# A hybrid conv / gated-linear / differential-attention layer in one kernel: convolution taps kept in emitted order and spread over both attentions, two empty steps more between channels, the first weight casts behind the squares, the low-rank weights loaded earlier

## The chip, the cores and the metric

One core of a Trainium2 chip. The metric is the device time of one execution in microseconds; lower is better. TensorE (PE) does the matrix products, VectorE (DVE) and ScalarE (ACT) the elementwise work, GpSimd (POOL) a few small operations and one queue of DMAs, SyncE (SP) issues nearly all other DMAs.

## What the kernel must compute

One layer of a streaming encoder on x of 1024 positions by 1024 channels, in float32:

```
h = rms_norm(x);  z = h @ W_in, split into the inputs of three mixers and three gates
A: u = a * sigmoid(gate); causal depthwise conv, 31 taps, over positions; LayerNorm; silu; @ w_pw
B: gated linear attention, 4 heads: logf = log_sigmoid(f_low @ w_f_up + b_f) / 16, with f_low 16 wide,
   cumulated in chunks of 64; within and across the chunks; rms_norm; * silu(og)
C: differential attention, 8 heads: softmax(q1 k1) - lam * softmax(q2 k2), chunk-causal,
   in blocks of 128 queries; @ v; rms_norm
x += (sigmoid gates on A, B, C) @ W_out;  x += SwiGLU FFN (2816 hidden);  rms_norm
```

## The kernel before

Each float32 product is three products of a faster format: an operand is split into a rounded high part (`wh`, an ACT cast, L121) and the rest (`wl`, a DVE subtraction, L122) by `hilo`, and `mm3` issues three matmuls (L125 to L127). The work runs in stages, one behind the other on PE: *head* (x is read, normalised, transposed into `h`, first two weight units), *blocks* (projections as seven-product block multiplications, until about 400 us), *gla* (attention B, until about 700 us), *diff* (attention C, head by head, until about 1190 us), the convolution's norm and projection, the output projection, the FFN.

The depthwise convolution is DVE work laid beside PE's. For each of 8 channel groups (`ct`), `conv_taps` emits 31 taps into one tile `acc` (128x1024, a single buffer): the first is a multiplication (L400), the others multiply and add (L402). Behind the last tap `acc` is stored to `c_d` by SP and added into a running sum `s_d` by an accumulating DMA on POOL's queue (L408). Because `acc` has one buffer, the first tap of the next channel waits until these two DMAs have read it. The taps' input comes back from memory `u_d`, written by `conv_in` (L413, L414) when a convolution unit of the blocks stage is finished.

What decides the order: the code calls `tick()` between small groups of matmuls (in the blocks stage every 6). A tick adds `TAP_RATE[stage]` to a counter; for each whole number in it `conv_step` advances `conv_taps` by one `yield`. Thus 31 steps are taps, and the `yield` behind the DMAs and the generator's end are steps that emit nothing. Then a scheduler orders each engine's instructions, and it may move one ahead of others on its engine where it takes the engine to be free, unless `tc.keep_in_program_order` holds it.

At the start SP issues x0, the constants, x1 to x3, the parameters, two weight tiles, x4 to x7. `x_scale(t)` squares an x tile on ACT (L323), forms its factor with a small DVE operation (`sm`, L131) and a POOL power (L132), and scales the tile on DVE (L325). `transposed` turns x0 to x3 into `h` (PE transposes L258, an ACT copy L260, a DVE subtraction L261).

`gla_begin` loads the two low-rank weights: `wf` (L449) and `wu3` (L451), casts `wf` into `wfx` (ACT L121 and L457) and multiplies `h` by it on PE (L466); `decay(0)` forms the gates: `fl`, a DVE minimum (L480), two ACT functions, a DVE subtraction (L483), eight DVE scans (L486), a DVE subtraction (L490). In the blocks stage `mix_finish` adds a finished PSUM block to an earlier one (DVE `t`, L937), which frees the bank for PE. In the diff stage `softmax(qb)` does for 128 queries: scores on PE (L686, L687), mask and maximum on DVE (L689 to L693), two exponentials on ACT (L695), then on DVE two reciprocals, a small product and the combination `p` (L700), which PE transposes; by the tables `LAG` and `SPACE` (L67, L68) the transposes stand 3 or 4 steps of a head's plan behind the scores, and the next block's scores 2 or 3 steps behind them.

Of the kernel before, what the change touches and what calls it, by code (L numbers as in the profile page):

```python
# [7 lines left out]
F32 = mybir.dt.float32  # L8
F32R = mybir.dt.float32r
U8 = mybir.dt.uint8  # L10
AF = mybir.ActivationFunctionType
ALU = mybir.AluOpType
# [4 lines left out]
P = 128  # L17
S = 1024
D = 1024
KT = D // P  # L20
NT = S // P
HALF = 512
# [16 lines left out]
P_DW, P_MIX, P_LNG, P_LNB, P_BF, P_GN, P_DN = 0, 248, 256, 264, 272, 276, 278  # L39
# [26 lines left out]
MIX0, MIX1 = 2, 18  # L66
LAG = (3, 3, 3, 3, 4, 4, 4, 4)  # L67
SPACE = (2, 2, 2, 2, 2, 2, 3, 3)  # L68
TAP_RATE = {"head": 0.0, "blocks": 0.42, "gla": 0.5, "diff": 0.72}


def body(nc, tc, I, out):
    x_d, w_d, wf_d, wfup_d, par_d, lq_d, cst_d, msk_d, ffg_d, fng_d = I
    vec, act, pe, pool, sp = nc.vector, nc.scalar, nc.tensor, nc.gpsimd, nc.sync
# [7 lines left out]
    cv = tc.alloc_tile_pool(name="cv", bufs=1)  # L82
    tp = tc.alloc_tile_pool(name="tp", bufs=8)
    sx = tc.alloc_tile_pool(name="sx", bufs=1)
    y2 = lambda name: yp.tile([P, HALF], F32, tag="y2", name=name)
# [25 lines left out]
    def bank():  # L111
        return ps.tile([P, HALF], F32, tag="pb", name="pb", bufs=4)

    def bank2():
        return ps.tile([P, 2 * HALF], F32, tag="sc", name="sc", bufs=2)

    def f(ap):
        return ap.bitcast(F32)

    def hilo(hi, lo, src):  # L120
        act.copy(hi, src)  # L121
        vec.tensor_tensor(out=lo, in0=src, in1=f(hi), op=ALU.subtract)  # L122

    def mm3(o, ah, al, bh, bl, start, stop, more=False):
        pe.matmul(o, ah, bh, start=start, stop=False, skip_group_check=more)  # L125
# [3 lines left out]
    def rstd(dst, ss, n, width):  # L129

        vec.tensor_scalar(out=dst, in0=ss, scalar1=1.0 / n, scalar2=EPS, op0=ALU.mult, op1=ALU.add)  # L131
        pool.tensor_tensor(out=dst, in0=dst, in1=mhalf[:, 0:width], op=ALU.pow)  # L132
# [5 lines left out]
    def raw_half(i, hf):  # L138
        raw = wp.tile([P, 1024], F32, tag="wr", name="wr", bufs=2)
        sp.dma_start(raw, w_d[i, hf])  # L140
        return raw

    def like(ap, src):
        return ap if len(src.shape) == 2 else ap.rearrange("p (k n) -> p k n", k=src.shape[1])

    def operand(src):
        wh = wp.tile([P, HALF], F32R, tag="wh", name="wh", bufs=8)
        wl = wp.tile([P, HALF], F32R, tag="wl", name="wl", bufs=8)
        hilo(like(wh, src), like(wl, src), src)
        return wh, wl  # L150

    def pieces(i):
        w = []
        ready.append(w)
        for hf in range(2):
            raw = raws0[hf] if i == 0 else raw_half(i, hf)
            for q in range(2):
                w.append(operand(raw[:, q * HALF:(q + 1) * HALF]))
                yield

    def wfinish():
        if state["gen"] is not None:
            for _ in state["gen"]:
                pass
            state["gen"] = None
# [7 lines left out]
    def wpiece():  # L173
        if state["gen"] is not None and next(state["gen"], 0) == 0:
            state["gen"] = None
# [50 lines left out]
    def taps(n):  # L226
        clock["conv"] = min(clock["conv"] + n, 2.0)
        while clock["conv"] >= 1.0 and conv_step():
            clock["conv"] -= 1.0

    def tick():
        if clock["now"] % 2 == 0:
            wpiece()
        clock["now"] += 1
        taps(TAP_RATE.get(clock["stage"], 0.5))
        while events and events[0][0] <= clock["now"]:
# [12 lines left out]
    def transposed(src, hh, hl, half, gcol, full=None):  # L249
        for k in range(KT):  # L250
            if half == 0 and k >= 4:
                if k % 2 == 0:
                    pt2 = bank2()
                pt = pt2[:, hs(k % 2)]
            else:
                pt = bank()
            for t in range(4):
                pe.transpose(pt[:, t * P:(t + 1) * P], src[t][:, k * P:(k + 1) * P], ident)  # L258
            g = par[:, gcol + k:gcol + k + 1]
            act.activation(hh[half][k // 4][:, k % 4, :], pt, AF.Copy, scale=g)  # L260
            vec.scalar_tensor_tensor(out=hl[half][k // 4][:, k % 4, :], in0=pt, scalar=g, in1=f(hh[half][k // 4][:, k % 4, :]),  # L261
                                     op0=ALU.mult, op1=ALU.subtract)
            if full is not None:
                full[k] = x2_("hf")
                act.activation(full[k], pt, AF.Copy, scale=g)
            yield k

    def bigset(pool_, tag, name):
        t = {(i, p): [pool_.tile([P, 4, HALF], F32R, tag=tag, name=f"{name}{p}{i}{j}") for j in range(2)]
             for i in range(2) for p in range(2)}  # L270
        return [[t[i, p] for i in range(2)] for p in range(2)]

    def hk(hset, half, k, c=slice(0, HALF)):
        return hset[0][half][k // 4][:, k % 4, c], hset[1][half][k // 4][:, k % 4, c]
# [19 lines left out]
    def hs(half):  # L294
        return slice(half * HALF, (half + 1) * HALF)


    hset = bigset(big, "big", "h")
# [2 lines left out]
    def tblock(name):  # L301
        T[name] = [tp.tile([P, 4, HALF], F32R, tag="tp", name=f"{name}{p}") for p in range(2)]

    xt2 = [tp.tile([P, 2, D], F32, tag="tp", name="xt") for _ in range(NT // 2)]
    xs = [xt2[t // 2][:, t % 2, :] for t in range(NT)]
    junks = tp.tile([P, 2, D], F32, tag="tp", name="junk")
    sp.dma_start(xs[0], x_d[0])
    sp.dma_start(cst, cst_d)
    for t in range(1, 4):
# [10 lines left out]

    def x_scale(t):
        ss, r = sm[:, t:t + 1], sm[:, 8 + t:9 + t]
        act.activation(junks[:, t % 2, :], xs[t], AF.Square, accum_out=ss)  # L323
        rstd(r, ss, D, 1)
        vec.tensor_scalar(out=xs[t], in0=xs[t], scalar1=r, scalar2=None, op0=ALU.mult)  # L325

    for t in range(4):
        x_scale(t)
    for _ in transposed(xs[0:4], *hset, 0, P_MIX):
        pass  # L330
    wfinish()


# [42 lines left out]
    for j in range(2):  # L376
        vec.tensor_tensor(out=lt[:, j * 64:(j + 1) * 64], in0=lq[:, j * 128:j * 128 + 64],
                          in1=lq[:, j * 128 + 64:j * 128 + 128], op=ALU.mult)
# [16 lines left out]
    def conv_taps(ct, up):  # L395
        acc = cv.tile([P, S], F32, tag="acc", name="acc", bufs=1)
        for j in range(TAPS):
            w = par[:, P_DW + ct * TAPS + j:P_DW + ct * TAPS + j + 1]
            if j == 0:
                vec.tensor_scalar(out=acc, in0=up[:, j:j + S], scalar1=w, scalar2=None, op0=ALU.mult)  # L400
            else:
                vec.scalar_tensor_tensor(out=acc, in0=up[:, j:j + S], scalar=w, in1=acc, op0=ALU.mult, op1=ALU.add)  # L402
            yield 1
        sp.dma_start(c_d[ct], acc)
        if ct == 0:
            sp.dma_start(s_d, acc)
        else:
            pool.dma_start(s_d, acc, accum_op=ALU.add)  # L408
        yield 1

    def conv_in(ct, half, sg, o):

# [25 lines left out]
    h2 = lambda name, dt=F32R: mix.tile([P, HALF], dt, tag="h2", name=name, bufs=8)  # L438
    G, C = {}, {}
# [3 lines left out]
    def gla_begin():  # L443
        ws, fl4, zs = q4("ws").bitcast(F32R), q4("fl").bitcast(F32R), q4("zs")
        C.update(wu=ws[0:96, 0:HALF], sst=ws[:, HALF:2 * HALF], fl=[fl4[0:96, hs(i)] for i in range(2)],
                 z2=zs[:, 0:HALF], sf=[zs[:, HALF + i * DV:HALF + (i + 1) * DV] for i in range(2)])
        wf = h2("wf", F32)[:, 0:KT * 16].rearrange("p (k n) -> p k n", k=KT)
        wu3 = h2("wu3", F32)[0:96, :]
        sp.dma_start(wf, wf_d)  # L449
        for j in range(6):  # L450
            sp.dma_start(wu3[16 * j:16 * j + 16, :], wfup_d)  # L451
        vec.memset(C["z2"], 0.0)
        yield 2
        wfx = mix.tile([P, KT, 96], F32R, tag="o4", name="wfx", bufs=2)
        hilo(wfx[:, :, 0:16], wfx[:, :, 16:32], wf)
        for j in range(1, 3):
            act.copy(wfx[:, :, 32 * j:32 * j + 32], f(wfx[:, :, 0:32]))  # L457
        wu, fl = C["wu"], C["fl"]
        act.copy(wu, wu3)
        vec.tensor_tensor(out=wu[64:96], in0=wu3[64:96], in1=f(wu[64:96]), op=ALU.subtract)  # L460
        yield 1
        for half in range(2):
            o = bank()[0:96, :]
            for k in range(KT):
                for p in range(2):
                    pe.matmul(o, wfx[:, k, :], hk(hset, half, k)[p], start=k + p == 0, stop=k + p == KT)  # L466
            act.copy(fl[half], o)
            vec.tensor_tensor(out=fl[half][32:64], in0=o[32:64], in1=f(fl[half][32:64]), op=ALU.subtract)
            yield 1
        yield from decay(0)  # L470
# [493 lines left out]
    NM = MIX1 - MIX0  # L964
# [15 lines left out]
            mb.make()  # L980
    conv_out(1)
    for n, p in order:
        for _ in range(2):
            if len(mb.made) < AHEAD:
                mb.make()
        mb.product(n, p)
        if mb.nxt == len(order) and len(mb.made) < 4 and state["n"] == MIX0:
            state["n"] = MIX1
            wstart()
        mb.after(n, p)  # L990
# [359 lines left out]
```

## Time and profile before

| | us |
|---|---|
| median of 3 runs (2113.55 to 2117.1) | 2115.08 |
| the profiled execution, its own time | 2115.08 |
| its span, first to last instruction | 2113.3 |
| PE busy | 2048.8 (97%) |
| DVE busy | 1447.5 (68%) |
| ACT busy | 892.8 (42%) |
| mean granted TensorE clock | 0.991 |

The profile's own execution is one of the three runs and the median of them; 1.8 us of it lie outside the span. Busy shares are means over the whole span; the stages differ, and the later sections read them stage by stage.

### The profile page before, as it was taken

To read this page: it belongs to the slowest core of one execution; us is meant where nothing else is said; L and a number is where in the kernel's file an instruction comes from. 1 tells how busy PE (TensorE), PEld (TensorE's weight loads), DVE (VectorE), ACT (ScalarE), POOL (GpSimd) and SP (SyncE) were. 2 spreads that over 40 slices of the span, in tenths; PEclk is the share of its full clock that TensorE was granted. 3 is DMA by queue.
4 is the path that set the end of the run, shared out by engine and by line. 5 is a ranking of instruction groups with operands and counts; after the bars stand their busy time and mean duration, and the time that the engine had idled before them with its cause. 6 is when DMAs were issued, how large, how long until landed. Compare 5 with 4: busy or idle time off the path is not lost.

```text
span 2113.3 us, 28321 instructions
## 1 busy us (share of the span) xinstructions
PE 2048.8 (97%) x10796; PEld 1751.7 (83%) x10796; DVE 1447.5 (68%) x2218; ACT 892.8 (42%) x1843; POOL 60.8 (3%) x64
## 2 busy tenths in 40 slices
PE   6999999899999999999999999999999999999998
PEld 4888787688888989898988888998888888888887
DVE  6999898889898555555554465468655555576766
ACT  6434333244453456556565462235433333432112
POOL 0000000000000000000000000000000000000000
PEclk9999999999999999999999999999999999999999
DMA  4232333421223533434332545342322222282111
GB/s 154 76 125 85 109 116 105 128 80 41 90 85 95 145 81 80 103 78 110 76 91 78 205 144 176 110 151 110 120 80 85 75 80 95 77 307 80 60 40 80
DMA packets 88538, 222.27 MB, mean 105 GB/s; under 512 B 10353, under 2 KB 21233, under 8 KB 88401
## 3 DMA queue, kind: packets, MB, share of 16 engines
q1 hardware_dynamic: 85664, 213.64, 31.2%
q0 software_dynamic: 2736, 6.82, 2.0%
q8 instruction: 85, 1.39, 0.3%
q14 instruction: 53, 0.43, 0.1%
HBM read 147.01 MB, written 54.53 MB: 95 GB/s over the span
## 4 chain that ended last, share of the span: by engine, by line
PE 68%; issue 15%; DVE 9%; DMA 3%; ACT 3%; POOL 1%; SPq 0%; DVEq 0%; POOLq 0%; ACTq 0%
PE pb L125 12%; PE pb L126 12%; PE pb L127 12%; PE sc L125 9%; PE sc L126 9%; PE sc L127 9%; DVE acc L402 3%; DMA s_d<-acc 2%; PE pb L722 2%; DVE wl L122 1%; PE sc L686 1%; PE sc L687 1%; POOL rs L132 1%; PE pb L711 1%; POOL sm L132 0%
## 5 line engine op out<-in xcount | busy, mean ns | idle before, releaser
L121 ACT CAST wh<-wr 128x512 fp32r<-128x512 f32 x315 | 193.5, 621 | 397.9 <-DVE x L1259 139.3
L122 DVE TENSOR_TENSOR wl<-wr,wh 128x512 fp32r<-128x512 f32 x315 | 214.0, 689 | 148.7 <-ACT wh L121 147.9
L402 DVE SCALAR_TENSOR_TENSOR acc<-up,par,acc 128x1024 f32<-128x1024 f32 x240 | 307.5, 1281 | 2.2
L125 PE MATMUL pb<-h,wh 128*128 128x512 f32 x704 | 281.4, 400 | 2.0 <-DVE h L261 2.0
L127 PE MATMUL pb<-h,wl 128*128 128x512 f32 x704 | 276.1, 392 | 0.0
L126 PE MATMUL pb<-h,wh 128*128 128x512 f32 x704 | 275.7, 392 | 0.0
L121 ACT CAST wh<-s 128x512 fp32r<-128x512 f32 x152 | 94.4, 621 | 229.9 <-PE sc L126 139.8
L1259 DVE TENSOR_TENSOR x<-x,pb 128x512 f32<-128x512 f32 x176 | 120.4, 685 | 61.4 <-PE pb L127 60.8
L127 PEld LDWEIGHTS pb<-h,wl 128*128 128x128 f32 x704 | 132.6, 188 | 29.0
L125 PEld LDWEIGHTS pb<-h,wh 128*128 128x128 f32 x704 | 132.7, 189 | 26.8 <-DVE h L261 2.2
L126 PEld LDWEIGHTS pb<-h,wh 128*128 128x128 f32 x704 | 132.8, 189 | 24.3 <-issue 0.2
L125 PE MATMUL pb<-wh,h 128*128 128x256 f32 x512 | 149.7, 292 | 0.4 <-DVE knl L122 0.4
L127 PE MATMUL pb<-wh,h 128*128 128x256 f32 x512 | 146.2, 285 | 0.0
L126 PE MATMUL pb<-wl,h 128*128 128x256 f32 x512 | 146.1, 285 | 0.0
L125 PE MATMUL sc<-bT,wh 128*128 128x512 f32 x352 | 137.0, 390 | 0.5 <-ACT bT L121 0.5
L126 PE MATMUL pb<-wl,mh 128*128 128x512 f32 x352 | 136.9, 389 | 0.0
L125 PE MATMUL pb<-wh,mh 128*128 128x512 f32 x352 | 136.9, 389 | 0.0
L127 PE MATMUL pb<-wh,ml 128*128 128x512 f32 x352 | 136.9, 389 | 0.0
L126 PE MATMUL sc<-bT,wh 128*128 128x512 f32 x352 | 136.8, 389 | 0.0
L127 PE MATMUL sc<-bT,wl 128*128 128x512 f32 x352 | 136.6, 389 | 0.0
L122 DVE TENSOR_TENSOR wl<-s,wh 128x512 fp32r<-128x512 f32 x152 | 104.0, 687 | 28.4 <-ACT wh L121 28.2
L125 PE MATMUL sc<-T,wh 128*128 128x512 f32 x256 | 101.6, 397 | 6.6 <-DVE t L937 6.6
(268 smaller groups left out, 4542.5 us busy)
## 6 DMA issues: line engine op xcount, KB each, us to landing
wr<-w_dram SPq DMA_DIRECT2D x176, 512.0 KB, 3.7
m_d<-t SPq DMA_DIRECT2D x44, 256.0 KB, 2.1
mr<-m_d SPq DMA_DIRECT2D x22, 512.0 KB, 5.5
k<-k SPq DMA_DIRECT2D x48, 128.0 KB, 3.2
kl<-kl SPq DMA_DIRECT2D x48, 128.0 KB, 3.0
xt<-x_dram SPq DMA_DIRECT2D x8, 512.0 KB, 8.4
up<-u_d SPq DMA_DIRECT2D x8, 512.0 KB, 5.5
gt_d<-t SPq DMA_DIRECT2D x16, 256.0 KB, 2.0
```

The costliest lines, as they stand in the source:

```text
L121: act.copy(hi, src)
L122: vec.tensor_tensor(out=lo, in0=src, in1=f(hi), op=ALU.subtract)
L125: pe.matmul(o, ah, bh, start=start, stop=False, skip_group_check=more)
L126: pe.matmul(o, ah, bl, start=False, stop=False, skip_group_check=more)
L127: pe.matmul(o, al, bh, start=False, stop=stop, skip_group_check=more)
L132: pool.tensor_tensor(out=dst, in0=dst, in1=mhalf[:, 0:width], op=ALU.pow)
L402: vec.scalar_tensor_tensor(out=acc, in0=up[:, j:j + S], scalar=w, in1=acc, op0=ALU.mult, op1=ALU.add)
L686: pe.matmul(sc[i][:, c], a["q"][i][:, t], a["k"][i][:, c], start=True, stop=False)
L687: pe.matmul(sc[i][:, c], a["q"][i][:, t], a["kl"][i][:, c], start=False, stop=True)
L711: pe.transpose(pt[:, i * P:(i + 1) * P], pd[:, (g0 + i) * P:(g0 + i + 1) * P], ident)
L722: pe.matmul(ov[:, 0:P], parts[k // 4][:, c], a["v"][:, k, :], start=k == 0, stop=k == nk - 1)
L1259: vec.tensor_tensor(out=xx, in0=xx, in1=o, op=ALU.add)
```

## The change

Four things. (1) The tap rates per tick become 0.45 (blocks), 0.45 (gla) and 0.82 (diff), and every tap is held in program order. (2) Behind each channel the generator yields three times where it yielded once. (3) At the start each x tile has a slot of its own, the squares' unused output goes to `acc`'s slot, and the four first weight casts with their subtractions are emitted one by one inside the loop over `transposed`, behind the four squares, and held there. (4) `wf` and `wu3` are loaded into `y2` tiles inside the blocks loop; `gla_begin` loses its loads and the `yield 2` behind them, and the `yield 1` behind the casts becomes `yield 3`.

```diff
-TAP_RATE = {"head": 0.0, "blocks": 0.42, "gla": 0.5, "diff": 0.72}
+TAP_RATE = {"head": 0.0, "blocks": 0.45, "gla": 0.45, "diff": 0.82}
...
-    def hilo(hi, lo, src):
-        act.copy(hi, src)
-        vec.tensor_tensor(out=lo, in0=src, in1=f(hi), op=ALU.subtract)
+    def stay(op):
+        tc.keep_in_program_order(op)
+
+    def hilo(hi, lo, src, pin=False):
+        a = act.copy(hi, src)
+        b = vec.tensor_tensor(out=lo, in0=src, in1=f(hi), op=ALU.subtract)
+        if pin:
+            stay(a)
+            stay(b)
...
-                w.append(operand(raw[:, q * HALF:(q + 1) * HALF]))
+                w.append(operand(raw[:, q * HALF:(q + 1) * HALF], i == 0))
...
-    xt2 = [tp.tile([P, 2, D], F32, tag="tp", name="xt") for _ in range(NT // 2)]
-    xs = [xt2[t // 2][:, t % 2, :] for t in range(NT)]
-    junks = tp.tile([P, 2, D], F32, tag="tp", name="junk")
+    xs = [tp.tile([P, 2, D], F32, tag="tp", name="xt")[:, 0, :] for _ in range(NT)]
+    junk = cv.tile([P, S], F32, tag="acc", name="junk", bufs=1)
...
     for t in range(4):
         x_scale(t)
-    for _ in transposed(xs[0:4], *hset, 0, P_MIX):
-        pass
+    wpiece()
+    for k in transposed(xs[0:4], *hset, 0, P_MIX):
+        if k % 2:
+            wpiece()
     wfinish()
...
+            stay(op)
             yield 1
         sp.dma_start(c_d[ct], acc)
...
-        yield 1
+        for _ in range(3):
+            yield 1
...
-        wf = h2("wf", F32)[:, 0:KT * 16].rearrange("p (k n) -> p k n", k=KT)
-        wu3 = h2("wu3", F32)[0:96, :]
-        sp.dma_start(wf, wf_d)
-        for j in range(6):
-            sp.dma_start(wu3[16 * j:16 * j + 16, :], wfup_d)
+        wf, wu3 = C["wf"], C["wu3"]
         vec.memset(C["z2"], 0.0)
-        yield 2
...
-        yield 1
+        yield 3
         for half in range(2):
...
     for n, p in order:
+        if (n, p) == (NM - 2, 0):
+            C["wf"] = y2("wf")[:, 0:KT * 16].rearrange("p (k n) -> p k n", k=KT)
+            C["wu3"] = y2("wu3")[0:96, :]
+            sp.dma_start(C["wf"], wf_d)
+            for j in range(6):
+                sp.dma_start(C["wu3"][16 * j:16 * j + 16, :], wfup_d)
```

The new lines shift the numbers: L400, L402 of before are L407, L409 after; L122 is L125, L323 is L328, L260 is L266, L700 is L704.

Place one, ACT at the start of the program (`wh` is a weight cast, `junk` a square, `h` the scaled copy of a transposed block). Before:

```order
L121 ACT_TABLE_LOAD
L121 CAST wh<-wr 128x512 x4
L323 ACTIVATE junk,sm<-xt 128x1024 x6
L260 ACTIVATE h_100<-pb,par 128x512 x4
L260 ACTIVATE h_101<-sc,par 128x512 x2
```

The same place in the changed kernel:

```order
L328 ACT_TABLE_LOAD
L328 ACTIVATE junk,sm<-xt 128x1024 x4
L124 CAST wh<-wr 128x512
L266 ACTIVATE h_100<-pb,par 128x512 x2
L124 CAST wh<-wr 128x512
L266 ACTIVATE h_100<-pb,par 128x512 x2
L124 CAST wh<-wr 128x512
L266 ACTIVATE h_101<-sc,par 128x512 x2
L328 ACTIVATE junk,sm<-xt 128x1024 x2
L266 ACTIVATE h_101<-sc,par 128x512
```

The four casts went from ahead of six squares to behind four, one for each pair of `h` copies; the squares of x4 and x5 stand ahead of the last `h` copies.

Place two, DVE in the gla stage, around the second head's decay chain (`t_3510`, later `t_3514`), where before a channel ended and the next began. Before:

```order
L402 SCALAR_TENSOR_TENSOR acc<-up_98,par,acc 128x1024
L122 TENSOR_TENSOR knl<-pb,knh 128x512
L480 TENSOR_SCALAR t_3510<-pb,par 128x512 x2
L400 TENSOR_SCALAR acc<-up_99,par 128x1024
L122 TENSOR_TENSOR vl<-pb,vh 128x512
L402 SCALAR_TENSOR_TENSOR acc<-up_99,par,acc 128x1024 x2
L483 TENSOR_TENSOR t_3510<-t_3510,t_3509 128x1024
L122 TENSOR_TENSOR knl<-pb,knh 128x512
L486 SCALAR_TENSOR_TENSOR t_3509<-cst,t_3510 128x128 x8
```

The same place in the changed kernel:

```order
L409 SCALAR_TENSOR_TENSOR acc<-up_99,par,acc 128x1024
L125 TENSOR_TENSOR wl<-wr,wh 128x512 x2
L125 TENSOR_TENSOR knl<-pb,knh 128x512
L484 TENSOR_SCALAR t_3514<-pb,par 128x512 x2
L125 TENSOR_TENSOR vl<-pb,vh 128x512
L487 TENSOR_TENSOR t_3514<-t_3514,t_3513 128x1024
L125 TENSOR_TENSOR knl<-pb,knh 128x512
L490 SCALAR_TENSOR_TENSOR t_3513<-cst,t_3514 128x128 x8
L494 TENSOR_TENSOR t_3514<-t_3513 128x1024
```

No tap is left inside the chain, and the channel's boundary, three rows wide before, is elsewhere. Of the 248 taps all stood ahead of the first `p` of the diff stage; now 155 do, and 10, 15, 10, 15, 14, 12 and 17 lie in heads 0 to 6 (counted from one head's first `p` to the next head's). Between a channel's last tap and the next first tap there were 3 to 9 DVE instructions; there are 7 to 31.

Place three, DVE in the diff stage, the softmax of a head's last block of queries (`sc` are scores, `st` the row statistics). Before:

```order
L689 MEMSET sc 64x64
L690 TENSOR_REDUCE st<-sc 128x1
L689 MEMSET sc 64x64
L690 TENSOR_REDUCE st<-sc 128x1
L697 RECIPROCAL st<-st 128x2
L698 TENSOR_SCALAR st<-st,lam 128x1
L700 SCALAR_TENSOR_TENSOR p<-sc,st,p 128x1024
```

The same place in the changed kernel:

```order
L409 SCALAR_TENSOR_TENSOR acc<-up_98,par,acc 128x1024
L693 MEMSET sc 64x64 x2
L694 TENSOR_REDUCE st<-sc 128x1 x2
L409 SCALAR_TENSOR_TENSOR acc<-up_98,par,acc 128x1024 x2
L701 RECIPROCAL st<-st 128x2
L702 TENSOR_SCALAR st<-st,lam 128x1
L704 SCALAR_TENSOR_TENSOR p<-sc,st,p 128x1024
```

Three taps now stand in and ahead of the chain that ends in `p`.

## Rows read from the trace of the kernel before

**Rows 1.** The page, busy time, share of the span, instructions of each engine.

```profile
PE 2048.8 (97%) x10796; PEld 1751.7 (83%) x10796; DVE 1447.5 (68%) x2218; ACT 892.8 (42%) x1843; POOL 60.8 (3%) x64
```

**Rows 2.** Waits of PE: tile waited at, releaser: us, times, longest.

```profile
PE pb L258 <- DVE sm L131: 17.7, 3, 17.2
PE sc L125 <- DVE t L937: 6.6, 2, 3.3
PE pb L466 <- ACT wfx L457: 6.5, 1, 6.5
PE sc L125 <- ACT ah L121: 4.1, 1, 4.1
```

**Rows 3.** Waits of DVE, same columns.

```profile
DVE acc L400 <- DMA s_d<-acc: 24.4, 5, 6.7
```

**Rows 4.** Windows: length, busy time (instructions) by engine, granted clock, DMA share.

```profile
100.00:200.00 100.00, 100.00 (x437) 81.39 (x437) 94.85 (x122) 41.19 (x71) 0.00 (x0) 1.00 0.31 103
240.00:404.00 164.00, 157.39 (x673) 127.68 (x672) 147.41 (x178) 58.89 (x102) 1.73 (x2) 0.98 0.34 110
412.00:426.00 14.00, 12.52 (x47) 8.81 (x48) 12.34 (x13) 5.19 (x8) 0.00 (x0) 0.87 0.20 61
426.00:700.00 274.00, 260.17 (x1660) 236.51 (x1659) 245.81 (x325) 121.43 (x253) 16.67 (x10) 0.98 0.26 78
660.00:700.00 40.00, 38.97 (x260) 35.46 (x259) 39.30 (x48) 14.03 (x33) 1.97 (x1) 1.00 0.32 99
720.00:1140.00 420.00, 415.87 (x2636) 372.98 (x2635) 227.73 (x459) 244.84 (x663) 22.34 (x19) 1.00 0.36 90
1020.00:1040.00 20.00, 19.29 (x132) 17.50 (x131) 14.83 (x30) 14.74 (x39) 1.78 (x2) 1.00 0.72 172
```

**Rows 5.** Timeline of DVE, blocks and gla: start, duration, instruction, [idle before].

```profile
241.53 0.75 DVE L400 TENSOR_SCALAR acc<-up,par 128x1024 f32<-128x1024 f32 x1 [3.69 <-DMA s_d<-acc]
...
249.64 0.69 DVE L937 TENSOR_TENSOR t<-sc,c 128x512 f32<-128x512 f32 x1
...
469.52 0.76 DVE L400 TENSOR_SCALAR acc<-up,par 128x1024 f32<-128x1024 f32 x1 [6.68 <-DMA s_d<-acc]
```

**Rows 6.** The page, costliest groups: busy us, mean ns of one, idle.

```profile
L402 DVE SCALAR_TENSOR_TENSOR acc<-up,par,acc 128x1024 f32<-128x1024 f32 x240 | 307.5, 1281 | 2.2
```

**Rows 7.** Line L408, the accumulating DMA, issue to landing.

```profile
DMA to landing us min/median/max: 6.0/8.2/9.0
```

**Rows 8.** Timeline at the start of gla, SP's queue and ACT.

```profile
408.89 0.33 SPq L449 DMA_DIRECT2D wf<-wf_dram  x1
...
410.90 0.30 ACT L121 CAST wfx<-wf 128x128 fp32r<-128x128 f32 x1 [9.93 <-DMA wf<-wf_dram]
```

**Rows 9.** Timelines of ACT, DVE and PE at the start.

```profile
12.07 2.42 ACT L121 CAST wh<-wr 128x512 fp32r<-128x512 f32 x4 [10.05 <-DMA wr<-w_dram]
14.39 1.05 ACT L323 ACTIVATE junk<-xt 128x1024 f32<-128x1024 f32 x1
...
22.15 2.42 ACT L260 ACTIVATE h<-pb,par 128x512 fp32r<-128x512 f32 x4 [1.42 <-PE pb L258]
...
20.83 0.75 DVE L325 TENSOR_SCALAR xt<-xt,sm 128x1024 f32<-128x1024 f32 x1 [0.66 <-POOL sm L132]
...
24.83 1.40 DVE L261 SCALAR_TENSOR_TENSOR h<-pb,par,h 128x512 fp32r<-128x512 f32 x2
...
25.62 0.50 PE L125 MATMUL pb<-h,wh 128*128 128x512 f32 x1 [1.98 <-DVE h L261]
```

**Rows 10.** Line L310, the loads of x1 to x3: issue ns, first and last start.

```profile
L310 SPq DMA_DIRECT2D xt<-x_dram x3: 424/432/432, 1.7 to 2.6; - x3
...
DMA to landing us min/median/max: 6.2/7.0/7.8
```

**Rows 11.** Timeline of POOL around the last tap.

```profile
689.06 1.97 POOL L132 TENSOR_TENSOR rs<-rs,mhalf 128x4 f32<-128x4 f32 x1 [35.87 <-DVE rs L131]
...
709.78 1.03 POOL L132 TENSOR_TENSOR rs<-rs,mhalf 128x4 f32<-128x4 f32 x1 [8.35 <-DVE rs L131]
```

More of the change, by code (lines that the diff above doesn't have):

```diff
@@ L144, in like, with operand @@
         return ap if len(src.shape) == 2 else ap.rearrange("p (k n) -> p k n", k=src.shape[1])
-    def operand(src):
+    def operand(src, pin=False):
         wh = wp.tile([P, HALF], F32R, tag="wh", name="wh", bufs=8)
         wl = wp.tile([P, HALF], F32R, tag="wl", name="wl", bufs=8)
-        hilo(like(wh, src), like(wl, src), src)
+        hilo(like(wh, src), like(wl, src), src, pin)
         return wh, wl
@@ L322, in x_scale @@
         ss, r = sm[:, t:t + 1], sm[:, 8 + t:9 + t]
-        act.activation(junks[:, t % 2, :], xs[t], AF.Square, accum_out=ss)
+        act.activation(junk, xs[t], AF.Square, accum_out=ss)
         rstd(r, ss, D, 1)
@@ L399, in conv_taps @@
             if j == 0:
-                vec.tensor_scalar(out=acc, in0=up[:, j:j + S], scalar1=w, scalar2=None, op0=ALU.mult)
+                op = vec.tensor_scalar(out=acc, in0=up[:, j:j + S], scalar1=w, scalar2=None, op0=ALU.mult)
             else:
-                vec.scalar_tensor_tensor(out=acc, in0=up[:, j:j + S], scalar=w, in1=acc, op0=ALU.mult, op1=ALU.add)
+                op = vec.scalar_tensor_tensor(out=acc, in0=up[:, j:j + S], scalar=w, in1=acc, op0=ALU.mult, op1=ALU.add)
+            stay(op)
             yield 1
```

## The prediction

> **What bounds the kernel now.** I read the page's busy times first: PE works 2048.8 us of a span of 2113.3 [rows 1], so 64.5 us are idle, and only these, with what the clock loses behind them, can be won by moving other engines' work. The list of PE's waits says where they lie [rows 2]: 17.7 us at the first transposes, 6.6 us in two waits for `t` in the blocks stage, 6.5 us for `wfx` at the start of gla, 4.1 us for `ah` in gla. In DVE's list one wait stands out: the first tap of a channel waits for the accumulating DMA, 24.4 us in five times [rows 3]. The timeline joins them [rows 5]: at 241.53 the first tap had held DVE idle for 3.69 us; DVE, in order, was then behind, and the `t` that PE needed came at 249.64, when PE had waited 3.3 us.
>
> The windows price each stage [rows 4]. From 100 to 200 us DVE is 94.85% busy and PE loses nothing: a full DVE costs nothing by itself while it is not late. From 240 to 404 us PE lacks 164 - 157.39 = 6.6 us and the granted clock is 0.98, which is another 0.02 x 164 = 3.3: **9.9 us**. From 404 to 426 us it lacks 6.5 for `wfx` and 14 - 12.52 = 1.5, and the clock at 0.87 over 14 us is 1.8 more: **9.8 us**. From 426 to 700 us it lacks 13.8, the clock at 0.98 is 5.5 more: **19.3 us**. From 720 to 1140 us it lacks 4.1 in 420.
>
> **The start.** Today ACT stands before its first cast until the weights land at 12.07; four casts, and the first square begins at 14.39 although x1 to x3 had all landed by 2.6 + 7.8 = 10.4 [rows 10]; the fourth tile is scaled at 20.83 and the first real matmul runs at 25.62 [rows 9]. In the new order the squares come first. The last tile is there at 10.4; a square takes 1.05 us [rows 9], with its read-out I put 1.2, so 11.6. On DVE the scaling of x2 and three small parameter operations stand ahead of x3's factor, which I put at 12.3; the wait for the power and the scaling were 0.66 and 0.75 us [rows 9], with the factor's small operation ahead 1.6, so x3 is scaled at 13.9. Before, ACT's first copy began 22.15 - (20.83 + 0.75) = 0.6 behind the scaling; then 0.6 for the copy (2.42 / 4), 0.7 for DVE's part (1.40 / 2) and little more: first matmul at about 15.9, a gain of at most 9.7 us. Not all of it stays. The copies for the second half of `h` come behind three casts, and the squares of x4 and x5 stand ahead of the last of them (two times 1.04 us), so PE, which needs 12 matmuls of about 100/437 = 0.23 us [rows 4] for the first half, runs dry once more, by 2 to 3 us. I take **-7.5** (bounds -4 and -9.7).
>
> **Blocks.** A tap is 1.28 us [rows 6]. The accumulating DMA lands 6.0 to 9.0 us after its issue [rows 7]. A tick is 6 matmuls, 1.4 us; from the step that issues the DMA to the next first tap there were 2 steps at 0.42 a tick, 2 / 0.42 x 1.4 = 6.7 us on paper, and the scheduler moved taps ahead of that. Now there are 4 at 0.45, 12 us, and taps stay. The effective rate hardly moves: 0.42 x 31/33 = 0.394 taps a tick before, 0.45 x 31/35 = 0.399 after, so DVE is as full as in the clean window. The price is the spacing alone, and DVE fills it with weight subtractions. I take **-9** of 9.9; one boundary has only seven DVE instructions in it, which at 0.7 us are 4.8 and leave 1 to 4 us of wait that DVE may or may not catch up (bounds -5 and -9.9).
>
> **Start of gla.** The issue of `wf` came at 408.89 and its cast at 410.90, so the load itself is 2.0 us on PE's way [rows 8]; SP stood before it behind a store of `u_d`, which waits for DVE's `t`, which was late behind a first tap. With the loads moved into the blocks stage, SP passes them long before, and the casts hang only on room in the pool and DVE. Two ticks of slack are added between the casts and their matmuls, and two removed before them, so PE's own order does not change much. Seven small DMAs stand on SP's queue earlier, about 3 us of issue, where it has room (DMA share 0.31, rows 4, at 100 to 200 us). I take **-7** of 9.8 (bounds -2, the load alone, and -9.8).
>
> **The rest of gla.** The largest term. Before, 248 taps stood ahead of diff's first `p`; now 155. Four channels, 124 taps, are through by the end of blocks in both, so gla keeps 31 of 124, and DVE's 245.8 us of 274 [rows 4] fall by 93 x 1.28 = 119 to about 127, under half. The waits of 4.1 us for `ah` (behind the first tap that waited 6.68 us, rows 5) and those behind decay chains mixed with taps should go. What stays is the chain's own length: eight scans, three subtractions and four ACT functions. I take **-14** of 19.3 (bounds -8 and -18).
>
> **Diff, the price.** The 93 taps land in heads 0 to 6, 119 us on DVE, whose 227.7 us of 420 become 347, 83%. The densest window has 14.83 of 20 [rows 4]; with its share, 5.7 us, it is full. Inside a softmax one to four taps delay `p` by 1.3 to 5.1 us, while PE has 3 or 4 steps of the head's plan to work on before it needs `p`. What a full DVE costs in an attention stage shows at 660 to 700 us: 39.30 of 40 busy with 20 taps in it, and PE lacks 1.0 us [rows 4]. The dense part is about half of each head; 7 heads at 0.5 us give **+3.5** (bounds 0 and, at one stall like that of 241 us in each head, 3.3 + 1.7 of clock, 7 x 5 = 35).
>
> A rule speaks against this part. Rows first: POOL's power `rs` on a 128x4 tile took 1.97 us among taps and 1.03 just behind the last one [rows 11], so taps slow POOL by 0.9 us each time. In diff one such power per head would cost 7 x 0.9 = 6 us if PE waited for it; it is consumed a head later, so I put nothing. The Trainium skill ("SBUF — State Buffer", section "Who interferes with whom") says that VectorE and GpSimd hold a shared port pair exclusively and the later one blocks; the trace agrees in direction, and by that rule with nothing to hide behind the sum would be 6 us worse, 2087.
>
> **Sum.** -7.5 - 9 - 7 - 14 + 3.5 = -34. The profiled execution's own time is 2115.08, which is also the median: **2081 us**.
>
> **Rivals.** *The stalls move to diff.* Softmax is a chain through DVE, ACT and DVE, and a tap of 1.28 us is longer than most of its links. For it: the dense windows become full, and taps no longer give way. Against it: 660 to 700 us. At one stall of 5 us in every second head the time is 2081 - 3.5 + 17 = 2095; at one in each head 2112, no change.
>
> *Slower than before.* The same mechanism twice a head: both dense blocks late, PE idle 3.3 and the clock 1.7 each time, 14 x 5 = 70 against 37.5 saved: 2148. It decides from 7.5 stalls on (one per head and a little). Against it: DVE keeps 17% free over the stretch.
>
> *The wait only moves.* The first taps after boundaries inside gla and diff still meet the DMA, and `wfx` still waits for the stores of `u_d`; the start gives 4. Then -4 - 6 - 2 - 10 + 3.5 = -18.5: 2097. For it: seven DVE instructions at one boundary, 7.7 us of landing on average.
>
> *More than forecast.* All bounds at their best: -9.7 - 9.9 - 9.8 - 18 = -47: 2068.
>
> **Chances.** Forecast (2072 to 2090) 0.60; better than that 0.10; the wait only moves 0.14; stalls in some heads 0.07; stalls in each, no change, 0.04; slower 0.05. The 80% range goes from 2066, the best case, to 2101, past the wait that moves and the stalls in half the heads. About 0.2% (4.2 us) is what a measurement can tell from no change: faster 0.91, same 0.04, slower 0.05.
>
> **What would show it.** First matmul near 16 us and a short second gap by 25; no idle of PE from 100 to 400 us and clock 1.00 there; the first taps' wait for the DMA under 8 us in all; `wfx` cast not waiting for a load; DVE about half busy in the gla stage and PE idle there under 6 us; from 720 to 1140 DVE near 347 us and PE idle 4 to 10. Wrong it would be if PE's list shows waits for `p` of more than 2 us per head with clock under 1.00, or if the first tap's wait stays above 15 us.

## The result

The changed kernel takes 2077.95 us (median of 4 runs, 2076.41 to 2080.82) against 2116.09 for the kernel before in the same comparison: the ratio of the means is 0.9823, 95% interval 0.9806 to 0.984. The forecast was 2081 us. The page of the changed kernel gives the busy times:

```profile
PE 2034.9 (98%) x10796; PEld 1741.6 (84%) x10796; DVE 1445.1 (70%) x2218; ACT 890.3 (43%) x1843; POOL 56.3 (3%) x64
```

The span is 2074.6 us, so PE idles 39.7 us where it idled 64.5 [rows 1]; its busy time fell by 13.9 us with the same 10796 matmuls; the mean granted clock rose from 0.991 to 0.999. PE's list of waits, the answer to [rows 2]:

```profile
PE pb L264 <- DVE xt L330: 10.4, 3, 9.6
PE sc L690 <- ACT p L699: 8.7, 4, 2.2
PE sc L690 <- DVE p L704: 1.6, 1, 1.6
...
PE sc L690 <- ACT osb L727: 1.4, 1, 1.4
...
PE pb L470 <- ACT wfx L461: 0.6, 1, 0.6
```

The waits for `t` and `ah` are nearly or quite gone, that for `wfx` fell from 6.5 to 0.6 us. The waits for `sc` in the diff stage grew: six waits, 11.7 us, where there had been six of 3.7 us together, by these lines of the kernel before:

```profile
PE sc L686 <- DVE p L700: 1.9, 3, 0.7
PE sc L686 <- ACT jk L725: 1.3, 2, 0.6
PE sc L686 <- ACT wh L121: 0.5, 1, 0.5
```

In DVE's list the first taps' wait for the accumulating DMA fell from 24.4 us [rows 3] to:

```profile
DVE acc L407 <- DMA s_d<-acc: 2.2, 1, 2.2
```

The windows that answer to [rows 4], cut where the same matmuls stand in the changed kernel (columns as there; 240 to 404, 404 to 426, 426 to 700 and 720 to 1140 us before):

```profile
233.84:387.77 153.93, 153.93 (x672) 125.25 (x671) 121.22 (x155) 59.12 (x102) 1.94 (x2) 1.00 0.37 117
387.77:402.57 14.80, 12.94 (x55) 9.13 (x54) 4.87 (x8) 6.12 (x10) 0.00 (x0) 1.00 0.16 50
402.57:654.37 251.80, 251.47 (x1660) 230.91 (x1659) 177.78 (x264) 122.07 (x255) 9.00 (x8) 1.00 0.25 75
674.06:1101.66 427.60, 415.89 (x2635) 372.38 (x2634) 332.42 (x553) 241.70 (x663) 25.90 (x23) 1.00 0.40 100
```

The four stretches took 164, 22, 274 and 420 us before; they take 153.9, 14.8, 251.8 and 427.6. In blocks PE lacks nothing and in gla 0.3 us, at clock 1.00; in diff it lacks 11.7 us where it lacked 4.1. DVE, 90% busy in the first and the third before (147.41 of 164, 245.81 of 274), is at 79% and 71%; in diff it rose from 54% to 78%. The rest of the span from diff's last matmul on is unchanged (933.9 us before, 933.6 after).

For each run the trace gives the starts of four matmul lines, and so the length of each stage. By the line numbers of the kernel before, the first is the first product (L125), the second the low-rank product (L466, so the wait for `wfx` counts to the stage ahead of it), the third the first scores (L686), the fourth the last of L722; all in us, of the profiled execution, with the measured ratio of all runs:

| kernel | first product | to gla | gla | diff | ratio to before |
|---|---|---|---|---|---|
| before | 25.6 | 386.7 | 313.9 | 453.2 | 1 |
| changed | 16.5 | 373.2 | 290.5 | 460.8 | 0.9823 |
| start as before | 26.1 | 370.8 | 290.6 | 463.9 | 0.9856 |
| one yield | 17.1 | 373.0 | 291.9 | 460.3 | 0.9825 |
| taps not held | 15.9 | 387.4 | 315.6 | 453.3 | 0.9955 |
| weights loaded in gla | 16.2 | 374.2 | 290.1 | 463.9 | 0.9827 |
| no taps in diff | 17.4 | 373.0 | 290.4 | 453.1 | 0.9764 |
| gla 0.60, diff 0.64 | 16.6 | 373.4 | 295.9 | 466.2 | 0.9846 |
| old rates | 16.0 | 372.1 | 296.8 | 470.2 | 0.9861 |
| before, taps held | 25.7 | 372.4 | 295.6 | 466.4 | 0.9893 |
| changed, again | 16.1 | 373.6 | 290.6 | 460.9 | 0.9817 |
| blocks 0.60 | 17.1 | 391.5 | 293.2 | 464.1 | 0.9912 |
| pause in each head | 16.9 | 373.1 | 291.4 | 456.8 | 0.9792 |
| both | 16.0 | 389.1 | 292.1 | 454.5 | 0.9864 |

### The profile page after: what moved, and what is told of

Read it like the earlier page. It is cut to its first block, busy times and chain, and to the rows that moved or that the text cites. A ratio compares the mean times of both kernels' runs of the same rounds, so it can differ in the third digit from the quotient of the medians.

```text
span 2074.6 us, 28309 instructions
## 1 busy us (share of the span) xinstructions
PE 2034.9 (98%) x10796; PEld 1741.6 (84%) x10796; DVE 1445.1 (70%) x2218; ACT 890.3 (43%) x1843; POOL 56.3 (3%) x64
## 4 chain that ended last, share of the span: by engine, by line
PE 79%; issue 9%; DVE 7%; ACT 2%; DMA 1%; POOL 1%; SPq 0%; DVEq 0%; POOLq 0%; ACTq 0%
PE pb L131 15%; PE pb L132 15%; PE pb L133 15%; PE sc L131 10%; PE sc L132 9%; PE sc L133 9%; PE pb L726 2%; DVE acc L409 1%; PE sc L690 1%; DVE wl L125 1%; PE sc L691 1%; PE pb L715 1%; DMA wr<-w_dram 1%; POOL sm L138 0%; POOL rs L138 0%
## 5 line engine op out<-in xcount | busy, mean ns | idle before, releaser
L125 DVE TENSOR_TENSOR wl<-wr,wh 128x512 fp32r<-128x512 f32 x315 | 214.6, 688 | 161.0 <-ACT wh L124 158.0
L409 DVE SCALAR_TENSOR_TENSOR acc<-up,par,acc 128x1024 f32<-128x1024 f32 x240 | 306.4, 1277 | 0.6
L131 PEld LDWEIGHTS pb<-h,wh 128*128 128x128 f32 x704 | 132.6, 188 | 25.6 <-ACT hf L271 1.2
L125 DVE TENSOR_TENSOR wl<-s,wh 128x512 fp32r<-128x512 f32 x152 | 103.7, 686 | 36.0 <-ACT wh L124 36.0
```

What stands on the lines that cost most here:

```text
L125: b = vec.tensor_tensor(out=lo, in0=src, in1=f(hi), op=ALU.subtract)
L409: op = vec.scalar_tensor_tensor(out=acc, in0=up[:, j:j + S], scalar=w, in1=acc, op0=ALU.mult, op1=ALU.add)
```

## The experiments

They ran in three groups of four, in this order; each ratio is to runs of the kernel before in the same group, whose median was 2115.74, 2119.27 and 2117.18 us, so ratios are compared across groups, not times.

**The start alone as before** (edit: the third part of the change reversed).

```diff
...
-    wpiece()
-    for k in transposed(xs[0:4], *hset, 0, P_MIX):
-        if k % 2:
-            wpiece()
+    for _ in transposed(xs[0:4], *hset, 0, P_MIX):
+        pass
...
```

> The changed kernel with its start alone as before (casts ahead of the squares, paired x tiles). If the start is worth what its own stretch shows (the ledger gives 7.7 us): 2078 + 7.7 = 2086 us, first real matmul at 25.6 us instead of 16.6. If the second half of h would have made PE wait anyway, or a later stage absorbs the shift: 2078 to 2080 us, although the first matmul is late.

Measured 2085.84 us, ratio 0.9856 (0.9841 to 0.9871). The start is worth 7 us. Its gain is 9.6 us at the first product (26.1 against 16.5) and 7.2 at the low-rank product (396.9 against 389.7); 2.4 us are lost on the way. The changed kernel's timeline of ACT and PE shows the start and two of the places where they go:

```profile
11.68 0.62 ACT L124 CAST wh<-wr 128x512 fp32r<-128x512 f32 x1 [0.42 <-DMA wr<-w_dram]
...
16.55 0.78 PE L131 MATMUL pb<-h,wh 128*128 128x512 f32 x1
...
33.08 0.65 PE L264 MATMUL pb<-cst,xt 128*128 128x128 f32 x4 [0.46 <-ACT hf L271]
...
35.97 0.50 PE L131 MATMUL pb<-h,wh 128*128 128x512 f32 x1 [0.99 <-ACT hf L271]
```

PE comes earlier to the second half of x, and ACT's copies `hf` are not ready: 1.4 us. Two more waits make up the rest, 0.56 us for ACT's `t` at 128 us and 0.35 us for DVE's `t` at 144 us.

**One yield behind a channel** (edit: `for _ in range(3): yield 1` becomes `yield 1`).

> The changed kernel with one yield behind each channel instead of three. Theory of the prediction (the spacing keeps the first tap from waiting for the accumulating DMA): the first taps' wait rises from 2.2 us to 15 to 24 us, PE waits for t in the blocks stage again, 2084 to 2087 us. Rival (holding the taps in order is what does it, the empty steps add nothing): wait under 8 us, 2076 to 2081 us.

Measured 2079.0 us, 0.9825 (0.9811 to 0.984): no difference to the changed kernel. The first taps wait for the DMAs 11.7 us, more than the rival's 8 and less than the 15 of the prediction's theory; the time is the rival's. The two waits lie at the end of gla and in diff:

```profile
673.65 0.76 DVE L407 TENSOR_SCALAR acc<-up,par 128x1024 f32<-128x1024 f32 x1 [7.38 <-DMA c_d<-acc]
...
790.89 0.75 DVE L407 TENSOR_SCALAR acc<-up,par 128x1024 f32<-128x1024 f32 x1 [4.34 <-DMA s_d<-acc]
```

In blocks no first tap waits for a DMA, with one yield as with three, and the stretch up to gla is 373.0 us long, as with three. The empty steps are worth nothing that can be measured; the prediction had put 9 us on them.

**Taps not held in order** (edit: `stay(op)` removed in `conv_taps`).

> The changed kernel with taps not held in program order; rates, three yields, start and weight loads stay changed. If holding the taps is what brings blocks and gla their gain: all taps lie ahead of the diff stage again, PE loses about 9 us in blocks and 20 us in gla and wins 7 back in diff, 2098 to 2102 us. If spacing and rates do it by themselves: 2078 to 2084 us.

Measured 2106.48 us, 0.9955 (0.994 to 0.997), worse than expected of the first theory by 4 us and far from the rival. The waits of the kernel before in blocks and gla are back, with three yields, new rates and early weights in place; the first taps' waits for the accumulating DMA too, 25.8 us in five. The 9 us that are left of the gain are about what the first product gained (15.9 against 25.6 us). PE's waits:

```profile
PE sc L131 <- DVE t L940: 6.9, 3, 3.5
PE pb L469 <- ACT wfx L460: 5.5, 1, 5.5
PE sc L131 <- ACT ah L124: 4.7, 1, 4.7
```

The windows with `acc`'s instructions alone tell why (columns: length, DVE busy and taps in it, POOL, clock, DMA share, GB/s; the windows lie at the same times, not at the same places of the program). First the kernel before, then the changed one, then this one:

```profile
100.00:390.00 290.00, 141.94 (x112) 2.67 (x3) 0.99 0.33 108
420.00:680.00 260.00, 126.97 (x101) 2.74 (x3) 0.97 0.24 75
700.00:1140.00 440.00, 0.15 (x1) 0.92 (x1) 1.00 0.37 94
```

```profile
100.00:390.00 290.00, 104.86 (x84) 1.94 (x2) 1.00 0.35 111
420.00:680.00 260.00, 66.71 (x53) 0.92 (x1) 1.00 0.27 80
700.00:1140.00 440.00, 116.69 (x93) 2.67 (x3) 1.00 0.37 94
```

```profile
100.00:390.00 290.00, 138.47 (x110) 2.80 (x3) 0.99 0.35 113
420.00:680.00 260.00, 127.24 (x102) 2.74 (x3) 0.98 0.26 80
700.00:1140.00 440.00, 0.00 (x0) 0.00 (x0) 1.00 0.37 94
```

Unheld, the scheduler pulled taps forward at either set of rates: 112 and 110 in blocks where 84 lie when they are held. Counted ahead of the low-rank product there are 133 taps in the kernel before, 132 in this run and 97 in the changed kernel. Holding them halves the taps in gla and takes a quarter out of blocks.

**The weights loaded in gla as before** (edit: the fourth part reversed).

> The changed kernel with the low-rank weights loaded in gla_begin as before. If the load stands on PE's path by its own length: PE waits for wfx 2 to 3 us instead of 0.6, 2080 us. If the whole old wait of 6.5 us came from the place of the loads: 2084 us. If the wait came only from DVE being late, which stays mended: no change, 2078 us.

Measured 2078.88 us, 0.9827 (0.981 to 0.9843): no change in time. PE waits 1.8 us for `wfx` instead of 0.6. With the loads early but the taps free it waited 5.5 (above). With the kernel before's loads and only the taps held it waits 1.9 us (the run with its taps held, below). Of the old wait of 6.5 us the load's place is worth 1.2; nearly all the rest was DVE's lateness.

**No taps in diff** (108 of 248 taps left out, so the convolution's sum lacks them).

```diff
+            if j and clock["stage"] == "diff":
+                yield 1
+                continue
```

> The changed kernel with the taps that fall into the diff stage left out, but for each channel's first (108 of 248 taps are missing, the convolution's sum is incomplete); rates and DMAs stay. It prices the taps in diff. If the waits of 1.4 to 2.2 us per head come from taps: they fall to 0.6 as before the change, 2078 - 7.6 = 2070 us. If they come from the shifted order of something else: 2076 to 2079 us.

Measured 2068.68 us, 0.9764 (0.9747 to 0.978). Diff takes 453.1 us, as before the change, and the waits there are back to 0.5 to 0.7 us. The taps in diff cost 7.7 us. By the marks of the table 91 of the missing taps had stood in diff and 17 at the end of gla, which is no shorter for it (290.4 against 290.5).

**More taps in gla, fewer in diff** (rates 0.60 and 0.64).

> The changed kernel with rates 0.60 in gla and 0.64 in diff instead of 0.45 and 0.82; 75 taps instead of 93 in heads 0 to 6, and 9 in head 7. If diff's loss goes with the number of taps and gla has room (DVE 71% busy there): diff wins 1 to 3 us, gla loses under 1, 2075 to 2077 us. If gla's gain hangs on DVE's room: gla loses 3 to 8 us, 2079 to 2085 us.

Measured 2085.05 us, 0.9846 (0.9832 to 0.9861), about 5 us slower than the changed kernel. Gla loses 5.4 us, as the second case had it; diff, with fewer taps, loses another 5.4, which neither case had. The whole diff stage of this run:

```profile
685.90:1152.10 466.20, 454.96 (x2807) 404.86 (x2806) 337.04 (x572) 265.23 (x713) 26.04 (x22) 0.99 0.38 95
```

PE idles 11.2 us in it, against 11.7 in the changed kernel; the loss is the clock's in this execution, the slowest of the four (0.99 over 466 us is about 5 us). So fewer taps did not make PE idle less.

**The old rates** (0.42, 0.50, 0.72).

> The changed kernel with the tap rates of before (0.42, 0.50, 0.72), the rest changed. If holding and spacing the taps do the work and the rates are fine tuning: 2076 to 2081 us. If the rates matter by themselves (diff's 0.82 costs, gla's 0.45 wins): one of the two stages moves by more than 3 us.

Measured 2089.01 us, 0.9861 (0.9846 to 0.9877), about 8 us slower; in the profiled execution, the slowest of its four, gla +6.3, diff +9.4. The rates matter, though the windows of 420 to 680 and 100 to 390 us hold about as many taps (54 and 80 against 53 and 84).

**The kernel before with its taps held, nothing else.**

> The kernel before with its taps held in program order and nothing else changed. If that alone spreads the taps and keeps DVE in time: blocks and gla win 9 + 20 us less diff's 7, 2093 to 2096 us. If without the two empty steps the first taps wait for the accumulating DMA: the wait is above 15 us and the time 2102 to 2116 us.

Measured 0.9893 (0.9878 to 0.9908), 2095.37 us. Up to gla 372.4 and gla 295.6 us: the call that holds the taps wins 14.3 and 18.3 us (4.6 of the first in the wait for `wfx`) and gives 13.2 back in diff. No first tap waits for the DMA, with one yield. In blocks there are as many taps as in the changed kernel (`acc`'s instructions alone, columns as above):

```profile
100.00:390.00 290.00, 105.52 (x84) 1.94 (x2) 1.00 0.34 112
```

**Where diff's loss sits.** The order of DVE's instructions, counted between the `p` of a head's third and that of its fourth query block, has 0, 2, 3, 1, 2, 2, 3, 0 taps in heads 0 to 7 of the changed kernel; PE's waits for `sc` are 2.12, 2.22, 1.40, 1.58, 2.11 and 2.22 us in heads 1 to 6, and none in head 0. The timeline of head 2 shows the chain:

```profile
809.92 1.28 DVE L409 SCALAR_TENSOR_TENSOR acc<-up,par,acc 128x1024 f32<-128x1024 f32 x1
811.29 1.22 DVE L409 SCALAR_TENSOR_TENSOR acc<-up,par,acc 128x1024 f32<-128x1024 f32 x1
...
812.43 1.22 DVE L697 TENSOR_REDUCE st<-sc 128x2 f32<-128x1024 f32 x1
813.68 0.69 ACT L699 ACTIVATE p<-sc,st 128x512 f32<-128x512 f32 x1 [1.04 <-DVE st L697]
...
814.65 0.65 ACT L699 ACTIVATE sc<-sc,st 128x512 f32<-128x512 f32 x1
...
815.96 0.75 DVE L704 SCALAR_TENSOR_TENSOR p<-sc,st,p 128x512 f32<-128x512 f32 x1
...
816.73 0.44 PE L690 MATMUL sc<-k,q 128*128 128x384 f32 x1 [2.22 <-ACT p L699]
```

There are two `sc` buffers (`bank2`). The fourth block, 512 keys, uses one; the fifth, 640 keys, needs both, so its second scores wait until the fourth block's exponentials and `p` have read theirs (the profile names an ACT `p`; DVE's `p`, which reads that buffer, ends at 815.96 + 0.75 = 816.71, just before the scores start). A tap in front of the fourth block's maximum (the reduction at 812.43) delays all of this. The last four runs test it.

**The changed kernel again, as their measure.**

> The changed kernel itself, as the measure for the three that share its chip: 0.982 of the kernel before, with waits of 1.4 to 2.2 us for sc at the fifth query block of heads 1 to 6.

Measured 2077.15 us, 0.9817 (0.9801 to 0.9834), with the same waits.

**More taps in blocks** (rate 0.60).

> The changed kernel with 0.60 instead of 0.45 taps a tick in blocks: 125 taps instead of 97 ahead of the start of gla, 62 instead of 93 in diff, none in heads 5 and 6. If blocks has room (DVE 82% busy) and diff's loss goes with the heads that hold taps: blocks unchanged, diff wins 2 to 3 us, 3 us faster than the changed kernel. If blocks' gain of 9 us came from the lower number of taps there: PE waits for t again, 2 to 9 us slower.

Measured 2097.64 us, 0.9912 (0.9897 to 0.9926): 20 us slower, far more than the second case had. In blocks, though held and spaced, the taps number as before the change; windows of this kernel, first all instructions, then `acc` alone:

```profile
100.00:390.00 290.00, 281.17 (x1205) 225.50 (x1204) 261.86 (x326) 109.22 (x191) 2.59 (x3) 0.99 0.32 106
```

```profile
100.00:390.00 290.00, 137.10 (x109) 2.59 (x3) 0.99 0.32 106
```

PE lacks 8.8 us in that stretch and 5.7 more for `wfx`, and the granted clock there is 0.99; its waits are for `wl` now, five times up to 2.2 us:

```profile
PE pb L133 <- DVE wl L125: 8.1, 5, 2.2
PE pb L470 <- ACT wfx L461: 5.7, 1, 5.7
```

No first tap waits for a DMA in that stretch, as two did before (at 241.53 [rows 5], and 4.47 us at 323). So the number of taps in the stage is enough to make DVE late, whatever their spacing.

**A pause in each head** (no taps from the third query block's scores to the fifth's).

```diff
-        while clock["conv"] >= 1.0 and conv_step():
+        while clock["conv"] >= 1.0 and not clock.get("hold") and conv_step():
...
             pend[i] = softmax(i)
+            clock["hold"] = i in (2, 3)
...
-"diff": 0.82
+"diff": 1.05
```

> The changed kernel without taps from a head's third to its fifth query block, at 1.05 instead of 0.82 taps a tick elsewhere in diff; 91 taps stay in heads 0 to 6. If the loss comes from taps between the p of the third and the p of the fourth block (2, 3, 1, 2, 2, 3 of them where PE waited 2.1, 2.2, 1.4, 1.6, 2.1, 2.2 us): waits fall to 0.6, 6 to 8 us faster than the changed kernel. If it comes from the number of taps in a head: no change, or 1 to 5 us slower.

Measured 2073.48 us (2073.02 to 2073.83), 0.9792 (0.9776 to 0.9808): 3.7 us faster than the changed kernel in the same group (2077.15, 2076.18 to 2081.14), with no overlap of the runs. With 91 taps still in heads 0 to 6 the waits for `sc` are under 1 us, and PE lacks 6.4 us in the diff stage where the changed kernel lacks 11.7:

```profile
681.40:1138.20 456.80, 450.40 (x2806) 400.71 (x2805) 343.94 (x579) 262.13 (x713) 24.95 (x22) 1.00 0.39 99
```

A part of the 6 to 8 us is spent on a new wait in head 0, where taps now stand in the first block's chain:

```profile
690.72 0.30 PE L715 MATMUL pb<-cst,p 128*128 128x128 f32 x1 [2.09 <-DVE p L704]
```

**Both** (0.60 in blocks, the pause, 0.9 in diff).

> Both: 0.60 in blocks, no taps from the third to the fifth query block, 0.9 elsewhere in diff; 62 taps in heads 0 to 5. If both reasons hold: as fast as the one without taps in diff, 7 to 8 us faster than the changed kernel. If room in blocks is lacking it is slower than the one with the pause alone.

Measured 2089.06 us, 0.9864 (0.9848 to 0.9881). Diff takes 454.5 us, within 1.4 of a diff stage without taps, and the stretch up to gla loses 15.5. The two effects are separate. This run and the one with 0.60 in blocks alone have 62 taps in diff each; with the pause PE idles 4.7 us there, without it 12.6 (first that run's diff stage, then this one's), so the place of the taps is the price and not their number:

```profile
701.80:1165.90 464.10, 451.45 (x2807) 401.75 (x2806) 313.49 (x550) 264.40 (x713) 25.92 (x22) 1.00 0.37 96
```

```profile
697.20:1151.70 454.50, 449.75 (x2806) 400.71 (x2805) 311.03 (x549) 262.72 (x713) 25.01 (x22) 1.00 0.38 98
```

## Why the prediction came out as it did

The time was right, by sizes that in part were right for another reason.

*The start* (-7.5): right in size; the run without it gives 7, and at 240 us of the kernel before the changed one is 6.2 us ahead. The first product came at 16.55 instead of 15.9, and the second dry spell of 2 to 3 us did not come: PE waits 0.7 us at 22.18. The 2.4 us that are lost go between 33 and 145 us, to ACT's copies and DVE.

*Blocks* (-9; 164 us became 153.9): right in size, wrong in reason. The failed step is "the effective rate hardly moves ... so DVE is as full as in the clean window ... the price is the spacing alone". The nominal rate hardly moves, but the scheduler had not kept to it: 112 taps lay in 290 us where 84 lie when held. Held taps alone win this (the kernel before with taps held), the empty steps nothing (one yield), and 109 held and spaced taps lose it again (blocks 0.60), with no first tap waiting there. The wait for the DMA at 241.53 [rows 5] was real, and PE's wait at 249.64 followed it, but it went with the taps that ran ahead: with taps free three empty steps did not end it, with taps held one is enough there. What it would cost by itself, in a DVE with room, no run shows in blocks; at the end of gla and in diff 11.7 us of it cost nothing that can be measured.

*The start of gla* (-7; 22 us became 14.8): the wait went as forecast, 5.9 us of it and the clock with it; the failed step is the cause given, the place of `wf`'s load. Putting the load back costs PE 1.2 us of wait and no measurable time; letting the taps free brings the wait back to 5.5 us with the load early. The row of SP's issue at 408.89 [rows 8] was read rightly as late, but the `u_d` stores ahead of it, and the room they free, are late because of DVE.

*The rest of gla* (-14; 274 us became 251.8, which is -22.2 and past the best bound of -18): mis-sized. Of the 13.8 us of idle 0.3 are left, and the clock is at 1.00. The premise of four channels through by the end of blocks in both kernels was wrong: 133 taps were through before, 97 are now. I counted that 31 taps stay in gla; 58 do, in a DVE busy 71% and not under half, and PE still loses nothing. Between the marks of the table the stage shrank by 23.4 us; 18.3 of them come from holding the taps at the old rates, and the new rates bring 5 to 6 more (changed against old rates).

*Diff* (+3.5): mis-sized, +7.6. Taps do delay `p`, as forecast. But PE did not wait to transpose `p`, for which the plan leaves 3 or 4 steps; it waited for the `sc` buffer that `p` frees, one block later, and that path the prediction had left out. The argument that 660 to 700 us shows what a full DVE costs [rows 4] was too kind, since a full DVE costs by where its work stands, at one place of a head, not by its share. POOL's power beside the taps changed nothing in the sum: in the changed kernel no tap stood beside one of the seven in diff (1.66 us each on 8 columns, as before), and PE never waited for one. The rule of the Trainium skill that was weighed there ("SBUF — State Buffer", "Who interferes with whom") is that VectorE and GpSimd share a port pair that only one of them holds at a time; the trace agrees where they meet: in gla two powers on 4 columns took 1.97 and 2.03 us beside taps and the other six 1.01 to 1.04, and in the run with the old rates one in diff took 2.74 us beside two taps.

The sum, -34, met -38.1 because gla's surplus of 8 outweighed diff's shortfall of 4; that the two errors partly cancelled was luck. The rival in which stalls move to diff holds in its mechanism, with about 1.3 us in each of six heads and, in the profiled execution, no fall of the clock. Of the signs that were named, two failed: DVE is 71% and not half busy in gla, and PE idles 11.7 us in diff and not 4 to 10.

## What to carry over

When a scheduler may move filler work forward, its rate in the code says nothing about where it lies; count it by stage in the trace before reasoning on rates. A wait in front of an engine that is 90% busy may be only where lateness shows; ask first what fills that engine. And filler work spread over a chained stage should be kept out of the few steps where buffers run out: here, keeping it out of one place of each head (PE idle 6.4 us instead of 11.7) won more than having fewer taps (11.2).

## What was not expected of the hardware

The same wait of PE costs the clock in one run and not in another. In the changed kernel, 2.11 us of idle in head 5 are followed by clock 1.00; in the run with the old start the same wait, shifted, is followed by 0.57 over 4 us. The two windows behind the wait, first of the changed kernel, then of that run:

```profile
988.00:992.00 4.00, 4.00 (x33) 4.00 (x34) 4.00 (x6) 1.68 (x4) 0.00 (x0) 1.00 0.87 175
```

```profile
996.00:1000.00 4.00, 4.00 (x23) 4.00 (x22) 4.00 (x6) 1.67 (x4) 0.00 (x0) 0.57 0.93 224
```

With as much DVE work in the four microseconds PE issues 23 matmuls instead of 33, and 0.43 of 4 us is 1.7 us. The same run has a second such stretch behind the wait in head 6 (0.57 from 1054 to 1058 us). The two are the 3 us by which diff is longer in that run and, with falls in the same two heads, in the one with the weights loaded in gla (463.9 against 460.8), a difference that is not theirs by their edits.

In the traces of all runs PE waited 2.1 to 2.9 us 33 times in diff. At the end of 14 of these waits the clock fell to half (1.2 of 2.4 GHz) for a stretch, and nowhere else in diff; the four waits of 2.3 us and more were all among them, and 10 of the 29 of 2.1 to 2.2 us. What decides it for those 29 these runs do not settle.

This also explains most of the 9.4 us that the old rates cost diff in their profiled execution:

```profile
684.90:1155.10 470.20, 454.69 (x2806) 404.80 (x2805) 350.13 (x584) 264.19 (x713) 27.05 (x23) 0.99 0.38 98
```

PE idles 15.5 us there, 3.8 more than in the changed kernel (16 taps fall into head 7, with a wait of 2.9 us), and the clock of 0.99 is about 5 us more.
